# One PSUM bank for a head's sum and its transpose, and separate buffers for the two parts of the transposed weights

## The chip, the cores and the metric

The kernel runs on one core of one Trainium2 chip. The core has five engines with an instruction stream each: TensorE (PE in the rows; its weight loads are listed apart as PEld), VectorE (DVE), ScalarE (ACT), GpSimd (POOL) and SyncE (SP), which issues most of the transfers. An engine takes its instructions in the order in which they were laid down, and stands still where the next one waits for another engine. The metric is the device time of one execution in microseconds (us).

## The reference, cut to what matters

One layer of an encoder over 1024 tokens of width 1024: a norm, one input projection, two token mixers (retention in 8 heads, and sparse attention in 8 heads), an output projection with the residual, a gated per-layer embedding and a last norm. The change lies in the sparse attention, and in one place of the last stage that uses the same buffers. In the attention each token attends, per head, to the 256 keys that an indexer chose for it:

```python
    logits = (jnp.einsum('bthc,btkc->bthk', ql, c_sel)
              + jnp.einsum('bthr,btkr->bthk', qp, pe_sel)).astype(jnp.float32) * scale
    logits = jnp.where(sel_ok[:, :, None, :], logits, -jnp.inf)
    prob = jax.nn.softmax(logits, axis=-1).astype(c_kv.dtype)
    o_lat = jnp.einsum('bthk,btkc->bthc', prob, c_sel)
    return jnp.einsum('bthc,hcd->bthd', o_lat, w_uv)
```

The kernel doesn't gather. It computes the logits of all keys of a block, adds a bias that is hugely negative for keys not chosen, and multiplies the resulting weights with values projected beforehand (`VD`).

## The kernel before, in words

The attention works through blocks of 256 tokens, `i` = 3, 2, 1, 0, and in each block through 8 heads `h` (`attend`). A head of block `i` has 2i+2 key tiles of 128. Per head:

- **Logits** (L956, L957): two matmuls for each half of the tokens and each 512 keys go into a bank of the pair `lg`; VectorE adds the bias and takes the running maximum (L958), which releases that bank; ScalarE takes the exponential (L962). The result `lm` has tokens on the partitions.
- **Transposed weights** (`key_chunks`): for two key tiles at a time, three or four TensorE transposes (L979) put the weights, keys on the partitions now, into a bank of the pair `tp`. ScalarE copies them out rounded, the high part `th` (L985), and VectorE subtracts that from the bank, which leaves the low part `tl_` (L986). Both parts lie in one tile `t2`, of which there are two. So the copy of a chunk waits until the tile of the chunk two before it has no reader left, and its last reader is the last L1015 of that chunk.
- **The sum** (`by_dim`, blocks 3, 2 and 1): for each key tile one matmul with the high part (L1014) and one with the low part (L1015), all added up in a bank of the pair `oo`, of which they use the first 256 columns.
- **The transpose back**: ScalarE copies the sum out as `os` (L1017), TensorE transposes it in two halves (L1020) into the other bank of the pair `oo`, and VectorE reduces that into `od` (L1021). Since each head takes two banks of a pair, the sum of every head lies in the same bank, and its transpose in the other.

Block 0 takes another way (`by_token`, L989, L1003), which needs only the high part and one bank.

Beside the attention run, in blocks 3 and 2, the units of the retention (`retention_unit`: L836 to L842, L849 to L910), which share ScalarE, VectorE and TensorE, and in block 1 and later the output projection (`project`, L1106 to L1126) and the split of its weights (`prep_w`, L1061 to L1065: load, ScalarE copy, GpSimd subtract). The last stage (`tail_in`, `tail_out`) handles 128 tokens at a time; `tail_in` transposes the residual in two halves and splits it (L1186 to L1190), the second half into a tile of the tag `t2`.

The order of the instructions on each engine isn't that of the program. A planner lays it out when the program is built, by priorities (`high_priority`) and by its own estimate of when each instruction can start and when a buffer comes free. The same planner makes an instruction wait for whatever reader or writer of a reused tile came last.

Of the kernel before, what the change touches and what calls it, by code (L numbers as in the profile page):

```python
# [8 lines left out]
F32 = mybir.dt.float32  # L9
FR = mybir.dt.float32r  # L10
# [4 lines left out]
AF = mybir.ActivationFunctionType  # L15
OP = mybir.AluOpType
# [137 lines left out]
def _body(ctx, nc, tc, ap, dbg):  # L154
    V, A, G, T, Y = nc.vector, nc.scalar, nc.gpsimd, nc.tensor, nc.sync

    def f(t):
        return t.bitcast(F32)
# [17 lines left out]
    def pool(name, **kw):  # L176
        return tc.tile_pool(name=name, bufs=kw.pop("bufs", 1), reuse_waits="tile", **kw)
# [129 lines left out]
    for k in range(NT):  # L307
        hi, lo = w1[k]
# [21 lines left out]
    def rsqrt(out, ssum, n, w):  # L330
        a = tiny.tile([128, 16], F32, name="rs_a")[:, :w]
        y = tiny.tile([128, 16], F32, name="rs_y")[:, :w]
        z = tiny.tile([128, 16], F32, name="rs_z")[:, :w]
        first = V.tensor_scalar(a, ssum, 1.0 / n, EPS, op0=OP.mult, op1=OP.add)  # L334
        G.tensor_tensor(out=y, in0=a, in1=mhalf[:, :w], op=OP.pow)  # L335
        V.tensor_tensor(out=z, in0=y, in1=y, op=OP.mult)
        V.tensor_tensor(out=z, in0=z, in1=a, op=OP.mult)
        V.tensor_scalar(z, z, -0.5, 1.5, op0=OP.mult, op1=OP.add)
        return first, V.tensor_tensor(out=out, in0=y, in1=z, op=OP.mult)
# [255 lines left out]
    def bank(name):  # L595
        turns[name] += 1
        tags = places[name]
        return psC.tile([128, 512], F32, name=name, tag=tags[turns[name] % len(tags)])
# [194 lines left out]
    dq_ = ctx.enter_context(pool("dsaq", bufs=3))  # L793
# [120 lines left out]
    dw_ = dw_s.enter_context(pool("dsaw", side="right", bufs=2))  # L914
# [25 lines left out]
    def attend(i, h):  # L940
        q, od, den = blocks[i]
        q, ql = q[h]
        mxv = tiny.tile([128, 4], F32, name="mxv")
        pt = []
        for a in range(2):
            j = 2 * i + a
            w = 128 * (j + 1)
            tsl = slice(128 * a, 128 * a + 128)
            lm = dw_.tile([128, S], F32, name="lm", bufs=4)
            mx = mxv[:, a:a + 1]  # L950
            part = mxv[:, 2 + a:3 + a]
            for n, c0 in enumerate(range(0, w, 512)):
                c1 = min(w, c0 + 512)
                kk = KK[h][:, 512 * n:512 * n + 512]
                lg = lg_tile()[:, :c1 - c0]
                T.matmul(lg, q[:, tsl], kk[:, :c1 - c0], start=True, stop=False)  # L956
                T.matmul(lg, ql[:, tsl], kk[:, :c1 - c0], start=False, stop=True)  # L957
                V.tensor_tensor_reduce(out=lm[:, c0:c1], in0=lg, in1=bias[:, OFF[j] + c0:OFF[j] + c1], scale=1.0,  # L958
                                       scalar=-3.0e38 if c0 == 0 else part, op0=OP.add, op1=OP.max,
                                       accum_out=part if c1 < w else mx)  # L960
            V.tensor_scalar(mx, mx, -0.125, None, op0=OP.mult)  # L961
            A.activation(lm[:, :w], lm[:, :w], AF.Exp, bias=mx, scale=0.125, accum_out=den[:, a, h:h + 1])  # L962
            pt.append(lm)
        if i < 1:
            by_token(i, h, pt, od)
        else:
            by_dim(i, h, pt, od)

    def key_chunks(pt, s0, last, split):
        tp = bank("tp")  # L970
        cols = []
        o = 0
        for s in (s0, s0 + 1):
            ks_ = slice(128 * s, 128 * s + 128)
            c0 = o
            for a in range(2):
                if last and s == s0 + 1 and a == 0:
                    continue
                T.transpose(tp[:, o:o + 128], pt[a][:, ks_], ident)  # L979
                o += 128  # L980
            cols.append((s, c0, o))
        t2 = dw_.tile([128, 2, 512], FR, name="t2")
        th, tl_ = t2[:, 0], t2[:, 1]
        if split:
            A.activation(th[:, :o], tp[:, :o], AF.Copy)  # L985
            V.tensor_tensor(out=tl_[:, :o], in0=tp[:, :o], in1=f(th)[:, :o], op=OP.subtract)  # L986
        else:
            th = f(t2)[:, s0 // 2 % 2]
            A.activation(th[:, :o], tp[:, :o], AF.Copy)  # L989
        return [(s, c0, c1, th, tl_) for s, c0, c1 in cols]  # L990

    def by_token(i, h, pt, od):
        ot = bank("oo")[:, :256].rearrange("p (a c) -> p a c", a=2)
        cols = [x for s0 in range(0, 2 * i + 2, 2) for x in key_chunks(pt, s0, s0 == 2 * i, False)]
        for a in range(2):
            mms = []
            for s, c0, c1, th, tl_ in cols:
                if s > 2 * i + a:
                    continue
                c = slice(c1 - 256 + 128 * a, c1 - 128 + 128 * a)  # L1000
                mms += [(th[:, c], s)]
            for n, (t, s) in enumerate(mms):
                T.matmul(ot[:, a], t, f(VD[s])[:, h].rearrange("p l d -> p (l d)"), start=n == 0, stop=n == len(mms) - 1)  # L1003
        V.tensor_reduce(od[:, :, h], ot.rearrange("p a (l d) -> p a d l", l=2), AX.X, OP.add)

    def by_dim(i, h, pt, od):
        ot = bank("oo")[:, :256]
        n_s = 2 * i + 2
        for s0 in range(0, n_s, 2):
            for s, c0, c1, th, tl_ in key_chunks(pt, s0, s0 == 2 * i, True):  # L1010
                q0 = 256 - (c1 - c0)
                v2 = VD[s][:, h].rearrange("p l d -> p (l d)")
                end = s == n_s - 1
                T.matmul(ot[:, q0:], v2, th[:, c0:c1], start=s == 0, stop=False, skip_group_check=end)  # L1014
                T.matmul(ot[:, q0:], v2, tl_[:, c0:c1], start=False, stop=s >= n_s - 2, skip_group_check=end)  # L1015
        os_ = dw_.tile([128, 512], F32, name="os")[:, :256]
        A.activation(os_, ot, AF.Copy)  # L1017
        tbp = bank("oo").rearrange("p (j d) -> p j d", d=128)
        for a in range(2):
            T.transpose(tbp[:, a], os_[:, 128 * a:128 * a + 128], ident)  # L1020
        V.tensor_reduce(od[:, :, h], tbp[:, 0:2].rearrange("p j (l d) -> p j d l", l=2), AX.X, OP.add)  # L1021
# [146 lines left out]
    def tail_in(j):  # L1168
        xt = dw_.tile([128, D], F32, name="xt", tag="lm", bufs=4)
        Y.dma_start(xt, d_xb[j])  # L1170
        sq = dw_.tile([128, D], F32, name="sqx", tag="od")
        s1 = tiny.tile([128, 1], F32, name="s1")
        A.activation(sq, xt, AF.Square, accum_out=s1)
        r1 = tiny.tile([128, 1], F32, name="r1")
        rsqrt(r1, s1, D, 1)
        V.tensor_scalar(r1, r1, 0.5, None, op0=OP.mult)
        pr = rp_.tile([128, 2, 128], F32, name="pr", tag="gt")
        Y.dma_start(pr, ap["pT"][:, 128 * j:128 * j + 128].rearrange("(k p) t -> p k t", p=128))
        p2 = rp_.tile([128, 2, 2, 128], FR, name="p2", tag="og")
        A.activation(p2[:, 0], pr, AF.Copy)  # L1180
        G.tensor_tensor(out=p2[:, 1], in0=pr, in1=f(p2)[:, 0], op=OP.subtract)
        hi, lo = [], []
        for q in range(2):
            pt = bank("tp")
            for k in range(4):
                T.transpose(pt[:, 128 * k:128 * k + 128], xt[:, 512 * q + 128 * k:512 * q + 128 * k + 128], ident)  # L1186
            x2 = (dw_.tile([128, 2, 512], FR, name="xT", tag="t2") if q else
                  dq_.tile([128, 2, 512], FR, name="xT", tag="ql"))
            A.activation(x2[:, 0], pt, AF.Copy)
            V.tensor_tensor(out=x2[:, 1], in0=pt, in1=f(x2)[:, 0], op=OP.subtract)  # L1190
            for k in range(4):
                hi.append(x2[:, 0, 128 * k:128 * k + 128])
                lo.append(x2[:, 1, 128 * k:128 * k + 128])
        return xt, sq, r1, p2, hi, lo

    def per_layer(p2):
# [5 lines left out]
    def tail_out(j, xt, sq, r1, p2, hi, lo):  # L1202
# [33 lines left out]
        for eng, c in ((A, slice(0, 512)), (Y, slice(512, 1024))):  # L1236
            eng.dma_start(ap["out"][128 * j:128 * j + 128, c], xt[:, c])

    ready = tail_in(order[0])
    for n, j in enumerate(order):  # L1240
        after = tail_in(order[n + 1]) if n + 1 < NT else None
        tail_out(j, *ready)
        ready = after
# [16 lines left out]
```

## Time and profile before

| | |
|---|---|
| median of 3 runs | 807.86 us (806.78 to 809.04) |
| the profiled execution's own time | 805.41 us |
| its span, first to last instruction | 803.6 us |
| mean granted TensorE clock | 0.979 of full speed |
| busy: PE, DVE, ACT, POOL | 754.4, 582.0, 469.4, 311.9 us |

The span and the engines' times are those of one profiled execution; what lies around the span in it is 805.41 - 803.6 = 1.8 us. The attention with the retention beside it runs from about 395 to 522 us after the span's start, the attention with the projection beside it from there to about 640 us, and the last stage to the end.

### The profile page before, as it was taken

How to read it: one execution, taken by the hardware profiler on the slowest of the kernel's cores; microseconds unless marked ns; L12 is line 12 of the kernel's file. 1: busy time of each engine (PE TensorE's matmuls, PEld its weight loads, DVE VectorE, ACT ScalarE, POOL GpSimd, SP SyncE). 2: the span in 40 equal slices, each digit the busy share in tenths (PEclk: the TensorE clock that was granted, in tenths of full speed). 3: DMA queues.
4: the chain of work that ended last, by engine and by line, in shares of the span. 5: the costliest groups of instructions: out<-in, count | busy, mean ns of one | idle time of the engine just before them, and what ended most of it. 6: DMA issues, size and time to landing. Idle time of an engine off the chain costs nothing.

```text
span 803.6 us, 12584 instructions
## 1 busy us (share of the span) xinstructions
PE 754.4 (94%) x4415; PEld 656.1 (82%) x4415; DVE 582.0 (72%) x1254; ACT 469.4 (58%) x1025; POOL 311.9 (39%) x237
## 2 busy tenths in 40 slices
PE   9999699989999999998999989799999899999995
PEld 6888599879888887997888879588788687888885
DVE  4968489999997999999879778755754633255344
ACT  6543466729997899963756656744754321333232
POOL 2918325455666434710046557630312230411000
PEclk9999899999999999999999999999999999999998
DMA  9414815323333224604525454654533662131201
GB/s 317 122 28 127 240 48 131 91 55 94 117 117 119 80 66 135 210 28 131 131 66 153 159 150 115 207 174 108 178 123 91 220 211 95 61 112 66 79 26 53
DMA packets 60831, 97.11 MB, mean 121 GB/s; under 512 B 5376, under 2 KB 32384, under 8 KB 60768
## 3 DMA queue, kind: packets, MB, share of 16 engines
q1 hardware_dynamic: 57152, 89.76, 36.5%
q10 hardware_dynamic: 3616, 6.55, 2.3%
q8 instruction: 35, 0.57, 0.3%
q14 instruction: 28, 0.23, 0.1%
HBM read 67.06 MB, written 29.23 MB: 120 GB/s over the span
## 4 chain that ended last, share of the span: by engine, by line
PE 53%; DVE 20%; issue 11%; DMA 7%; POOL 4%; ACT 3%; SPq 2%; POOLq 0%; ACTq 0%; DVEq 0%
PE lg L1165 6%; PE ra L1165 5%; PE big L326 3%; PE big L325 3%; PE big L324 3%; PE oo L1165 3%; DVE res L657 3%; PE nb L502 2%; PE nb L503 2%; PE nb L504 2%; DMA qk<-d_f 2%; PE ra L1122 2%; PE ra L1123 2%; PE ra L1124 2%; DVE sc L484 2%
## 5 line engine op out<-in xcount | busy, mean ns | idle before, releaser
L237 POOL TENSOR_TENSOR wlo<-wraw,whi 128x512 fp32r<-128x512 f32 (+1 forms) x58 | 88.8, 1547 | 66.2 <-ACT whi L236 66.2
L673 ACT ACTIVATE ajunk<-key,cthr 128x1024 bf16<-128x1024 int16 (+5 forms) x96 | 95.5, 994 | 14.8 <-DVE key L634 10.5
L502 PE MATMUL nb<-whi,xhi 128*128 128x256 f32 x256 | 74.8, 295 | 8.8 <-ACT nst L506 8.8
L657 DVE TENSOR_SCALAR_CACHE_REDUCE res<-key,athr 128x384 f32<-128x384 int16 (+5 forms) x96 | 75.5, 786 | 2.1
L503 PE MATMUL nb<-wlo,xhi 128*128 128x256 f32 x256 | 74.1, 291 | 0.7 <-POOL wlo L237 0.7
L504 PE MATMUL nb<-whi,xlo 128*128 128x256 f32 x256 | 73.5, 290 | 0.0
L335 POOL TENSOR_TENSOR rs_y<-rs_a,mhalf 128x1 f32<-128x1 f32 (+1 forms) x26 | 26.2, 1006 | 101.5 <-DVE rs_a L334 98.7
L962 ACT ACTIVATE lm<-lm,mxv 128x896 f32<-128x896 f32 (+3 forms) x64 | 49.5, 775 | 25.6 <-DVE mxv L961 25.4
L985 ACT ACTIVATE t<-tp 128x512 fp32r<-128x512 f32 (+1 forms) x72 | 39.3, 556 | 39.5 <-PE oo L1015 27.1
L502 PEld LDWEIGHTS nb<-whi,xhi 128*128 128x128 f32 x256 | 50.7, 199 | 10.8 <-ACT nst L506 9.7
L325 PE MATMUL big<-xlo,whi 128*128 128x512 f32 x144 | 56.1, 389 | 0.0
L324 PE MATMUL big<-xhi,whi 128*128 128x512 f32 x144 | 55.7, 389 | 0.0
L986 DVE TENSOR_TENSOR t<-tp,t 128x512 fp32r<-128x512 f32 (+1 forms) x72 | 45.6, 640 | 14.0 <-ACT t L985 13.6
L326 PE MATMUL big<-xhi,wlo 128*128 128x512 f32 x144 | 55.7, 390 | 0.0
L484 DVE SCALAR_TENSOR_TENSOR sc<-rel,wi,sc 128x1024 f32<-128x1024 f32 (+5 forms) x42 | 51.0, 1213 | 5.8 <-ACT rel L480 3.1
L958 DVE CUSTOM_DVE_ANT_0 lm<-lg,bias 128x512 f32<-128x512 f32 (+2 forms) x64 | 36.7, 587 | 23.5 <-PE tp L979 12.0
L503 PEld LDWEIGHTS nb<-wlo,xhi 128*128 128x128 f32 x256 | 50.8, 199 | 1.9 <-POOL wlo L237 1.3
L504 PEld LDWEIGHTS nb<-whi,xlo 128*128 128x128 f32 x256 | 50.4, 198 | 0.6
L979 PE MATMUL tp<-cst,lm 128*128 128x128 f32 x288 | 48.1, 277 | 0.6 <-DVE rs_a L334 0.3
L1014 PE MATMUL oo<-t,vd 128*128 128x256 f32 (+1 forms) x144 | 40.5, 293 | 7.7 <-ACT os L1017 6.2
L1219 DVE SCALAR_TENSOR_TENSOR sqx<-sqx,oo 128x512 f32<-128x512 f32 (+1 forms) x17 | 10.5, 653 | 49.6 <-PE oo L1165 35.0
L236 ACT ACTIVATE whi<-wraw 128x512 fp32r<-128x512 f32 (+1 forms) x58 | 34.9, 609 | 14.9 <-POOL cg L535 4.2
(492 smaller groups left out, 2423.5 us busy)
## 6 DMA issues: line engine op xcount, KB each, us to landing
wraw<-in_w_t SPq DMA_DIRECT2D x26, 256.0 KB, 2.7
wraw<-in_w_n SPq DMA_DIRECT2D x24, 256.0 KB, 2.6
d_f<-o SPq DMA_DIRECT2D x8, 512.0 KB, 3.9
qk<-d_f SPq DMA_DIRECT2D x8, 512.0 KB, 4.5
ql<-d_qs SPq DMA_DIRECT2D x16, 256.0 KB, 5.1
qh<-d_qs SPq DMA_DIRECT2D x32, 128.0 KB, 4.1
twr<-in_w_out SPq DMA_DIRECT2D x8, 512.0 KB, 5.4
xt<-in_x SPq DMA_DIRECT2D x8, 512.0 KB, 3.5
```

The costliest lines, as they stand in the source:

```text
L237: G.tensor_tensor(out=lo, in0=raw, in1=f(hi), op=OP.subtract)
L324: T.matmul(outs[h], wh, xhi[k][:, sl], start=k == 0, stop=False)
L325: T.matmul(outs[h], wh, xlo[k][:, sl], start=False, stop=False)
L326: last = T.matmul(outs[h], wl, xhi[k][:, sl], start=False, stop=k == 7)
L484: V.scalar_tensor_tensor(dst, rel[:, :w], wi[:, i, h:h + 1], dst, op0=OP.mult, op1=OP.add)
L502: T.matmul(pb[:, a % 2], xhi[k][:, tsl], wh, start=k == 0, stop=False)
L503: T.matmul(pb[:, a % 2], xhi[k][:, tsl], wl, start=False, stop=False)
L504: last = T.matmul(pb[:, a % 2], xlo[k][:, tsl], wh, start=False, stop=k == 7)
L657: V.tensor_scalar(junk, src[:, KS[i]], thr[:, n:n + 1], 0.0, op0=op, op1=OP.add, accum_out=cnt[:, n:n + 1])
L673: A.activation(junk[:, :128 * (i + 1)], src[:, KS[i]], AF.Sign, bias=self.thr[:, n:n + 1], accum_out=cnt[:, n:n + 1])
L962: A.activation(lm[:, :w], lm[:, :w], AF.Exp, bias=mx, scale=0.125, accum_out=den[:, a, h:h + 1])
L1165: T.matmul(po[c.start // 512][:, c.start % 512:c.start % 512 + c.stop - c.start], a, b[:, c], start=k == 0 and m == 0, stop=k == n - 1 and ...
```

## The change

A head's sum and its transpose now lie in the two halves of one bank, so that successive heads take turns in the two banks of the pair `oo`. The tile `t2` becomes two: `th`, of which there are three, and `tl`, of which there are two. The tile `os` has half its size. The space per partition stays the same: t2 2 x 4 KB and os 2 x 2 KB were 12 KB; th 3 x 2 KB, tl 2 x 2 KB and os 2 x 1 KB are 12 KB. In the last stage the second half of the transposed residual takes its tiles from the tags `th` and `tl`. No computation is added or removed.

```diff
@@ key_chunks
-        t2 = dw_.tile([128, 2, 512], FR, name="t2")
-        th, tl_ = t2[:, 0], t2[:, 1]
+        th = tl_ = dw_.tile([128, 512], FR, name="th", bufs=3)
         if split:
+            tl_ = dw_.tile([128, 512], FR, name="tl")
             A.activation(th[:, :o], tp[:, :o], AF.Copy)
             V.tensor_tensor(out=tl_[:, :o], in0=tp[:, :o], in1=f(th)[:, :o], op=OP.subtract)
         else:
-            th = f(t2)[:, s0 // 2 % 2]
+            th = f(th)
             A.activation(th[:, :o], tp[:, :o], AF.Copy)
@@ by_dim
-        ot = bank("oo")[:, :256]
+        both = bank("oo")
+        ot = both[:, :256]
...
-        os_ = dw_.tile([128, 512], F32, name="os")[:, :256]
+        os_ = dw_.tile([128, 256], F32, name="os")
         A.activation(os_, ot, AF.Copy)
-        tbp = bank("oo").rearrange("p (j d) -> p j d", d=128)
+        tbp = both[:, 256:].rearrange("p (j d) -> p j d", d=128)
@@ tail_in
-            x2 = (dw_.tile([128, 2, 512], FR, name="xT", tag="t2") if q else
-                  dq_.tile([128, 2, 512], FR, name="xT", tag="ql"))
-            A.activation(x2[:, 0], pt, AF.Copy)
-            V.tensor_tensor(out=x2[:, 1], in0=pt, in1=f(x2)[:, 0], op=OP.subtract)
+            if q:
+                xh, xl = (dw_.tile([128, 512], FR, name="xT" + tag, tag=tag, bufs=n) for tag, n in (("th", 3), ("tl", 2)))
+            else:
+                x2 = dq_.tile([128, 2, 512], FR, name="xT", tag="ql")
+                xh, xl = x2[:, 0], x2[:, 1]
+            A.activation(xh, pt, AF.Copy)
+            V.tensor_tensor(out=xl, in0=pt, in1=f(xh), op=OP.subtract)
...
```

## Rows read from the trace of the kernel before

**Rows 1.** Busy time of each engine in three stretches: the attention beside the retention, the attention beside the projection, the last stage. Columns: stretch and its length, then busy us (and instructions) of PE, PEld, DVE, ACT and POOL, the granted clock, the DMA share, GB/s.
```profile
395.00:522.00 127.00, 112.85 (x820) 101.61 (x819) 103.02 (x262) 81.10 (x154) 70.80 (x67) 0.96 0.46 139
522.00:640.00 118.00, 113.16 (x695) 98.07 (x693) 67.25 (x206) 58.04 (x144) 24.56 (x16) 1.00 0.47 147
640.00:803.00 163.00, 154.26 (x714) 126.24 (x714) 66.54 (x169) 51.43 (x101) 30.62 (x30) 0.97 0.26 91
```

**Rows 2.** What TensorE's matmuls waited for between 355 and 645 us: who, for whom, us in total, times, the longest.
```profile
PE oo L1014 <- ACT os L1017: 6.2, 4, 3.2
PE lg L956 <- DVE mxv L958: 4.1, 5, 1.7
...
PE oo L1014 <- ACT t L985: 1.3, 2, 1.0
```

**Rows 3.** The instructions of the copy out, of the transpose back and of the reduction: count, then least, median and greatest ns of one, first and last start.
```profile
L1017 ACT ACTIVATE os<-oo x24: 373/379/388, 411.3 to 603.5; 128x256 f32<-128x256 f32 x24
...
L1020 PE MATMUL oo<-cst,os x48: 270/272/421, 412.8 to 608.1; 128*128 128x128 f32 x48
...
L1021 DVE TENSOR_REDUCE od<-oo x24: 407/416/426, 413.4 to 608.6; 128x128 f32<-128x256 f32 x24
```

**Rows 4.** The first of TensorE's four waits for `os`, in order of time: start, us, engine, line, operation; in brackets the idle time before it and who ended it.
```profile
407.58 0.59 ACT L985 ACTIVATE t<-tp 128x512 fp32r<-128x512 f32 x1
...
408.78 0.68 DVE L986 TENSOR_TENSOR t<-tp,t 128x512 fp32r<-128x512 f32 x1
...
410.82 0.60 ACT L985 ACTIVATE t<-tp 128x512 fp32r<-128x512 f32 x1
...
411.31 0.38 ACT L1017 ACTIVATE os<-oo 128x256 f32<-128x256 f32 x1
...
411.74 0.39 PE L1014 MATMUL oo<-t,vd 128*128 128x256 f32 x1 [1.51 <-ACT os L1017]
...
412.76 0.63 PE L1020 MATMUL oo<-cst,os 128*128 128x128 f32 x2
```

**Rows 5.** The second of them, the same way.
```profile
473.08 0.58 ACT L985 ACTIVATE t<-tp 128x512 fp32r<-128x512 f32 x1
...
473.55 0.38 ACT L1017 ACTIVATE os<-oo 128x256 f32<-128x256 f32 x1
...
473.99 0.39 PE L1014 MATMUL oo<-t,vd 128*128 128x256 f32 x1 [0.90 <-ACT os L1017]
...
474.68 0.38 PE L1020 MATMUL oo<-cst,os 128*128 128x128 f32 x2
```

**Rows 6.** The third of them.
```profile
509.69 0.58 ACT L985 ACTIVATE t<-tp 128x512 fp32r<-128x512 f32 x1
...
510.16 0.37 ACT L1017 ACTIVATE os<-oo 128x256 f32<-128x256 f32 x1
...
510.59 0.38 PE L1014 MATMUL oo<-t,vd 128*128 128x256 f32 x1 [0.61 <-ACT os L1017]
...
511.29 0.38 PE L1020 MATMUL oo<-cst,os 128*128 128x128 f32 x2
```

**Rows 7.** The fourth and longest, with what ScalarE did ahead of it.
```profile
516.52 1.06 ACT L1064 ACTIVATE wo3h<-twr 128x1024 fp32r<-128x1024 f32 x1 [2.89 <-DMA twr<-in_w_out]
517.48 0.58 ACT L985 ACTIVATE t<-tp 128x512 fp32r<-128x512 f32 x1
...
517.96 0.38 ACT L1017 ACTIVATE os<-oo 128x256 f32<-128x256 f32 x1
...
518.39 0.58 PE L1014 MATMUL oo<-t,vd 128*128 128x256 f32 x1 [3.22 <-ACT os L1017]
...
519.62 0.63 PE L1020 MATMUL oo<-cst,os 128*128 128x128 f32 x2
```

**Rows 8.** Stretches of 2 us around the first and the fourth of these waits; columns as in rows 1, the clock third from the end.
```profile
410.00:412.00 2.00, 0.49 (x5) 0.26 (x3) 1.79 (x2) 1.95 (x5) 2.00 (x2) 1.00 0.00 0
412.00:414.00 2.00, 2.00 (x11) 2.00 (x11) 1.46 (x5) 1.80 (x4) 1.04 (x1) 0.51 0.00 0
414.00:416.00 2.00, 2.00 (x14) 2.00 (x13) 1.42 (x5) 0.00 (x0) 0.51 (x2) 0.64 0.00 0
...
516.00:518.00 2.00, 0.00 (x0) 0.00 (x0) 0.00 (x0) 1.48 (x3) 0.35 (x1) 0.96 1.07 389
518.00:520.00 2.00, 1.61 (x8) 1.61 (x8) 1.11 (x4) 2.00 (x5) 2.00 (x1) 0.50 0.59 195
520.00:522.00 2.00, 2.00 (x13) 1.70 (x12) 1.28 (x4) 2.00 (x5) 1.75 (x2) 0.69 0.84 265
```

**Rows 9.** Waits of ScalarE and VectorE for the split of the transposed weights, between 395 and 522 us.
```profile
ACT t L985 <- PE oo L1015: 10.6, 9, 3.1
...
DVE t L986 <- ACT t L985: 3.9, 2, 2.4
```

**Rows 10.** The first of these waits between 522 and 582 us.
```profile
ACT t L985 <- PE oo L1015: 16.0, 8, 5.2
```

**Rows 11.** The latest reduction of a head against the sums that follow: the reduction of one head, the copy of the next head's sum, and the first matmul of the head after that.
```profile
590.91 0.43 DVE L1021 TENSOR_REDUCE od<-oo 128x128 f32<-128x256 f32 x1 [3.28 <-PE oo L1020]
591.04 0.38 ACT L1017 ACTIVATE os<-oo 128x256 f32<-128x256 f32 x1
...
594.80 0.29 PE L1014 MATMUL oo<-t,vd 128*128 128x256 f32 x1
```

More of the change, by code (lines that the diff above doesn't have):

```diff
@@ L1186, in tail_in @@
                 T.transpose(pt[:, 128 * k:128 * k + 128], xt[:, 512 * q + 128 * k:512 * q + 128 * k + 128], ident)
-            x2 = (dw_.tile([128, 2, 512], FR, name="xT", tag="t2") if q else
-                  dq_.tile([128, 2, 512], FR, name="xT", tag="ql"))
-            A.activation(x2[:, 0], pt, AF.Copy)
-            V.tensor_tensor(out=x2[:, 1], in0=pt, in1=f(x2)[:, 0], op=OP.subtract)
+            if q:
[5 more added lines that the diff above has]
+            V.tensor_tensor(out=xl, in0=pt, in1=f(xh), op=OP.subtract)
             for k in range(4):
-                hi.append(x2[:, 0, 128 * k:128 * k + 128])
-                lo.append(x2[:, 1, 128 * k:128 * k + 128])
+                hi.append(xh[:, 128 * k:128 * k + 128])
+                lo.append(xl[:, 128 * k:128 * k + 128])
         return xt, sq, r1, p2, hi, lo
```

## The prediction, made before the changed kernel was run

> **What bounds the kernel now.** I read the busy times by stage first. In all three stages that the change touches, TensorE is the engine that is nearly always busy: 112.85 of 127 us beside the retention, 113.16 of 118 beside the projection, 154.26 of 163 in the last stage [rows 1]. VectorE comes second, and only in the first of them is it close: 103.02 of 127. So a gain must come out of TensorE's idle time, and 127 - 112.85 = 14.2 us of it lie in the first stage. Next I read what TensorE waited for. The largest entry is the wait for `os`: 6.2 us in four waits, the longest 3.2; the waits for VectorE's logits follow with 4.1, and those for the high part `th` with 1.3 [rows 2]. The four waits are all in the first stage, and each has the same shape [rows 4 to 7]: TensorE has finished the sum of one head and stands at the first L1014 of the next, which can't write since ScalarE has not yet copied the old sum out of the one bank that all sums use. ScalarE is late not because the copy is long (379 ns) [rows 3] but because it stands behind other work in ScalarE's stream; in the fourth case behind a weight copy that itself waited 2.89 us for its load [rows 7].
>
> **The change part by part.** No instruction is added, removed or made longer: the copy still reads 128x256, the transposes and the reduction are the same. Only waits change, and then the order that the planner makes of them. The sum is in these steps.
>
> *The bank.* The next head's sum now has the other bank, so its L1014 no longer waits for `os`. But L1020, the transpose of the old head, still does, and in the present order it stands behind the first five matmuls of the next head. So the wait isn't gone; it moves to L1020, and to any L1014 whose `th` isn't ready, since `th` comes from the same ScalarE. I therefore price each of the four by when L1020 could start, with the order unchanged.
> - First [rows 4]: the inputs of the first four matmuls are there (`th` ended at 408.17, `tl` at 409.46). They run in the 1.51 us in which TensorE now idles. The fifth needs the `th` that ends at 411.42, L1020 the `os` that ends at 411.69. L1020 starts at about 411.75 and not at 412.76: 1.0 us.
> - Second [rows 5]: `th` ends at 473.66, `os` at 473.93; L1020 starts at 473.95 and not at 474.68: 0.7 us.
> - Third [rows 6]: `os` ends at 510.53; L1020 starts at about 510.6 and not at 511.29, but no more can be won than the 0.61 us of idle time: 0.6 us.
> - Fourth [rows 7]: `th` ends at 518.06, `os` at 518.34; L1020 starts at 518.4 and not at 519.62: 1.2 us. The rest of the 3.22 us stays, because ScalarE is still behind the weight copy.
>
> Together 1.0 + 0.7 + 0.6 + 1.2 = 3.5 us. From below: nothing, if each gain is taken back at the next wait for VectorE. From above: all 6.2 us, if the planner uses its freedom to put the stalled copies earlier.
>
> *The bank's release.* A bank is now held until VectorE's reduction of the head, not only until the copy, and the head after next needs it. The latest reduction ended at 591.34, and the first sum that would need that bank began at 594.80 [rows 11]: 3.5 us to spare, so I price it at nothing. If that cover goes, each head pays up to the reduction's 416 ns [rows 3] and its handover.
>
> *Three `th`, two `tl`.* ScalarE sat 10.6 us in nine waits for the last L1015 of an older chunk [rows 9]. With a third `th` it can copy one chunk further ahead, so most of these waits leave ScalarE. They don't vanish: `tl` still has two buffers, so VectorE's subtraction waits for the same L1015, and the bank in `tp` is not free before it. Behind it in VectorE's stream stand the logits L958, whose lateness TensorE already pays with 4.1 us [rows 2]. After the release only the subtraction (0.68 us) is left to do and not copy and subtraction (0.59 + 0.68) [rows 4], so a chunk is ready up to 0.6 us sooner. TensorE waited only 1.3 us for `th` in all [rows 2]. Bounds: a gain of these 1.3 us, and a loss of up to the whole 10.6 us if all of it reached TensorE through VectorE. I take 0: VectorE has 127 - 103.02 = 24 us of idle time there to absorb it [rows 1], and 3.9 us of it is already spent on waiting for this `th` [rows 9]. Between 522 and 582 us ScalarE sat another 16.0 us [rows 10], in the stage in which TensorE hardly idles [rows 1]; nothing is won or lost there.
>
> *Block 0, the last stage, `os`'s size.* Block 0 uses one bank per head as before. The last stage gets a third buffer for the high part of half its tiles, where TensorE is busy 154.26 of 163 us [rows 1]. Nothing, unless that cover goes.
>
> *The clock.* After the first wait the granted clock fell to 0.51 and 0.64 in two stretches of 2 us, after the fourth to 0.50 and 0.69 [rows 8]: 2.4 GHz became 1.2 for part of them. Lost: 2 x 0.49 + 2 x 0.36 = 1.7 us, and 1.61 x 0.50 + 2 x 0.31 = 1.4 us. Before both falls TensorE had been idle for the better part of a stretch [rows 8]. In the unchanged order some 2.7 us of the fourth idle time and 0.8 us of the first stay, so I leave both falls in the sum.
>
> The Trainium skill, "TensorE: Matmul & The Clock Gate", Part 1, says that throttled is the default state and that activity releases it. By that rule the first fall, whose idle time is broken up and shortened, would go as well, and the sum would be 3.5 + 1.7 = 5.2 us; by the rows it is 3.5.
>
> The profiled execution took 805.41 us, 1.8 us of it around the span of 803.6, and lies 2.45 us under the median of the runs, 807.86. Taken off each: 801.9 and **804.4 us**. What differs by under 0.3% (2.4 us) can't be told from no change.
>
> **The rivals.**
> - *More than the sum.* The planner, no longer held by the bank and by `t2`, lays `os` and `th` ahead of the weight copy. Then all 6.2 + 1.3 us of waits go, and with them both falls of the clock: 7.5 + 1.7 + 1.4 = 10.6 us, 797.3 us. For it: the planner decides by when a buffer is free, and that is what changes. Against it: it didn't foresee the 2.89 us load in front of the weight copy, and still won't.
> - *Nothing that can be told.* L1020 and its followers are earlier, but TensorE then waits the longer for VectorE's logits (4.1 us now), so that 2 to 3 of the 3.5 us are given back: 806 to 808 us. The third `th` does nothing either, since two banks in `tp` and two `tl` still limit the chunks in flight. For it: VectorE is busy 81% of that stage.
> - *Slower: the wait moves to VectorE.* What ScalarE sat out (10.6 us) VectorE sits out, with the logits behind it, and TensorE stands at L956. If two thirds reach TensorE, 7.1 - 3.5 = +3.6 us, 811.5 us; it ends slower by over 2.4 us from 5.9 of the 10.6 us on. For it: VectorE's stream is fuller than ScalarE's (103 against 81 us) [rows 1]. Against it: its 24 us of idle time.
> - *Slower: the bank's release.* If the planner lays reductions late, the head after next waits for each. At 0.42 us for the 22 heads that have one two before them, 9.2 - 3.5 = +5.7 us, 813.6 us. It decides from 5.9 us in all, 0.27 us a head. Against it: the 3.5 us to spare.
>
> The Trainium skill, "PSUM — Partial Sum Buffer", § PSUM bank collisions, wants engines kept apart by bank, not by address. By that rule a sum that shares a bank with a transpose stays locked until VectorE has read the transpose, the mechanism of this last rival; it would give 813.6 us, where rows 11 give 804.4.
>
> **How the numbers follow.** Forecast (gain 2.4 to 5.2 us, 802.7 to 805.4): 0.35. More: 0.15. Nothing: 0.28. VectorE: 0.17. Bank: 0.05. So faster 0.35 + 0.15 = 0.50, the same 0.28, slower 0.22. The range runs from 797.5, which leaves out the far half of the second case, to 812, which leaves out the bank's rival and the far end of VectorE's: about 2 in 10 in all. The forecast's own range is 802.7 to 805.4. The largest thing that I can't see is the planner: every order after the first changed tile can shift, on SyncE's and GpSimd's queues too (the loads of `qk` and of the weights, the weight splits), and one new stall like the fourth with its fall of the clock costs 3.2 + 1.4 = 4.6 us, which alone would turn the forecast.
>
> **What would show it.** Right: the entry L1014 for `os` gone from TensorE's waits, a smaller one of L1020 for `os` in its place; ScalarE's 10.6 us for L1015 down to 3 or less, and a new wait of VectorE's L986 for L1015; TensorE's idle time in that stage down by 3 to 4 us from 14.2; the last stage equally long. Wrong: TensorE's wait for the logits (L956) grown by 5 us or more, a new wait of L1014 for the reduction L1021, a fall of the clock at a place where there was none, or a stage other than this one that changes its length by over 2 us.

## The result, and the profile after

The changed kernel takes 796.14 us (median of 4 runs, 792.77 to 798.29) where the kernel before took 807.32 beside it: a ratio of 0.985, interval [0.980, 0.990]. That is 11.2 us less, three times the 3.5 us of the sum, and 1.4 us below the foot of the range. A few executions of the kernels in this document were disturbed and took far longer; the medians and ratios leave them out, and a dash in the tables stands where the profiled execution was one of them.

The profiled execution took 798.29 us, the longest of its runs; its span is 796.1 us, 7.5 shorter than before. The busy times of the first stage, in the columns of [rows 1]:

```profile
395.00:522.00 127.00, 117.95 (x870) 107.89 (x870) 106.13 (x285) 87.97 (x169) 76.18 (x69) 0.97 0.50 152
```

Between 395 and 522 us TensorE executes 870 matmuls where it executed 820, and idles 9.1 us where it idled 14.2. Stretches bound to the work say more than stretches bound to the clock on the wall. From the first transposes of the weights (L979) to the last matmul of the retention (L893), before and after:

```profile
397.50:494.90 97.40, 89.31 (x672) 82.18 (x673) 80.24 (x195) 58.46 (x112) 52.28 (x55) 0.96 0.40 120
```

```profile
399.70:490.60 90.90, 86.37 (x673) 80.21 (x673) 77.96 (x196) 58.53 (x112) 52.49 (x56) 1.00 0.42 123
```

This part is 6.5 us shorter: 3.6 us less idle time, and a granted clock of 1.00 where it was 0.96. The clock's part of that isn't the change's alone: in a second profiled execution of the same changed kernel, 796.0 us long, the clock fell once in this part (0.50 and 0.65 between 414 and 418 us), and it took 92.4 us with a clock of 0.98. What TensorE waits for between 355 and 645 us, against [rows 2]:

```profile
PE ra L1123 <- DVE mTl L1114: 3.3, 1, 3.3
PE oo L1015 <- ACT th L985: 3.3, 3, 2.1
...
PE lg L956 <- DVE mxv L958: 0.4, 1, 0.4
```

The wait for `os`, 6.2 us, is gone without a remainder: no L1021 (the transpose back, L1020 before) waits for it either. The wait for the logits fell from 4.1 to 0.4 us, which nothing in the sum foresaw. How a head's end looks now (start, us, engine, line; the copy out is L1018, the reduction L1022):

```profile
471.74 0.39 ACT L1018 ACTIVATE os<-oo 128x256 f32<-128x256 f32 x1
...
472.25 0.28 PE L1015 MATMUL oo<-th,vd 128*128 128x256 f32 x1
...
472.54 1.10 PE L854 MATMUL ra<-vt,kt 128*128 128x128 f32 x8
...
474.20 0.38 PE L1021 MATMUL oo<-cst,os 128*128 128x128 f32 x2
...
477.23 0.41 DVE L1022 TENSOR_REDUCE od<-oo 128x128 f32<-128x256 f32 x1
```

The copy ends at 472.13, and the transposes that need it are laid so far behind that TensorE reaches them at 474.20, after a stretch without a gap. In [rows 4 to 7] they came right behind five matmuls that themselves stood behind the copy. The order of the instructions has changed, not only the waits. This head is one of 24: from the end of the copy to the transposes it takes 0.05 to 6.1 us in the changed kernel, 0.27 to 6.5 us in the one before.

### The profile page after: what moved, and what is told of

It reads as the page before. It is cut to its first block, busy times and chain, and to the rows that moved or that the text cites. A ratio compares the mean times of both kernels' runs of the same rounds, so it can differ in the third digit from the quotient of the medians.

```text
span 796.1 us, 12587 instructions
## 1 busy us (share of the span) xinstructions
PE 751.8 (94%) x4415; PEld 655.7 (82%) x4415; DVE 580.5 (73%) x1254; ACT 469.1 (59%) x1025; POOL 312.2 (39%) x237
## 4 chain that ended last, share of the span: by engine, by line
PE 60%; DVE 21%; DMA 8%; issue 4%; ACT 3%; SPq 1%; POOL 1%; ACTq 0%; POOLq 0%; DVEq 0%
PE lg L1166 6%; DVE res L657 5%; PE ra L1166 5%; PE ra L1125 3%; PE ra L1123 3%; PE ra L1124 3%; PE oo L1166 3%; DMA qk<-d_f 2%; PE tp L979 2%; PE nb L502 2%; PE nb L503 2%; PE nb L504 2%; DVE sc L484 2%; PE ra L893 1%; PE lg L956 1%
## 5 line engine op out<-in xcount | busy, mean ns | idle before, releaser
L985 ACT ACTIVATE th<-tp 128x512 fp32r<-128x512 f32 (+1 forms) x72 | 39.8, 557 | 39.8 <-PE tp L979 38.5
L335 POOL TENSOR_TENSOR rs_y<-rs_a,mhalf 128x1 f32<-128x1 f32 (+1 forms) x26 | 28.0, 1076 | 86.7 <-DVE rs_a L334 83.7
L502 PEld LDWEIGHTS nb<-whi,xhi 128*128 128x128 f32 x256 | 50.4, 198 | 10.9 <-ACT nst L506 9.7
L986 DVE TENSOR_TENSOR tl<-tp,th 128x512 fp32r<-128x512 f32 (+1 forms) x72 | 45.7, 639 | 5.9 <-ACT th L985 3.4
L979 PE MATMUL tp<-cst,lm 128*128 128x128 f32 x288 | 48.2, 277 | 0.3 <-DVE tl L986 0.3
L1015 PE MATMUL oo<-th,vd 128*128 128x256 f32 (+1 forms) x144 | 41.4, 296 | 3.3 <-ACT th L985 3.3
L236 ACT ACTIVATE whi<-wraw 128x512 fp32r<-128x512 f32 (+1 forms) x58 | 34.9, 609 | 15.2 <-POOL cg L535 5.0
L1016 PE MATMUL oo<-tl,vd 128*128 128x256 f32 (+1 forms) x144 | 40.3, 313 | 0.1
```

The source lines that it names most:

```text
L502: T.matmul(pb[:, a % 2], xhi[k][:, tsl], wh, start=k == 0, stop=False)
```

## The experiments

Three theories to begin with: **A**, the bank does it; **B**, the third `th` does it; **C**, neither by itself, but the order that the planner lays around them. In the tables, "idle + clock" is worked out from stretches of 2 us, from the first L979 to the end of the span: TensorE's idle time, plus its busy time times one minus the granted clock, summed. Each figure is from one profiled execution; the changed kernel's two agree. For the kernel before the sum is 28.3 + 6.1 = 34.4 us, for the changed one 22.8 + 4.4 = 27.2.

**Halves of the change.** The whole again; the bank alone (buffers as before); the buffers alone (two banks a head as before); the whole with two `th`.

```diff
 e1_bank_only, against the kernel before
-        ot = bank("oo")[:, :256]
+        both = bank("oo")
+        ot = both[:, :256]
-        tbp = bank("oo").rearrange("p (j d) -> p j d", d=128)
+        tbp = both[:, 256:].rearrange("p (j d) -> p j d", d=128)
 e2_buffers_only, against the changed kernel
-        both = bank("oo")
-        ot = both[:, :256]
+        ot = bank("oo")[:, :256]
-        tbp = both[:, 256:].rearrange("p (j d) -> p j d", d=128)
+        tbp = bank("oo").rearrange("p (j d) -> p j d", d=128)
 e3_two_th, against the changed kernel
-        th = tl_ = dw_.tile([128, 512], FR, name="th", bufs=3)
+        th = tl_ = dw_.tile([128, 512], FR, name="th", bufs=2)
```

> The changed kernel once more, beside the three kernels that take it apart. All theories: 0.985 of the kernel before, 793 to 798 us.

> The kernel before with the bank's half of the change alone: sum and transpose in one bank, heads taking turns; t2 and os as before. Theory A (the bank is the cause: the sum of the next head no longer waits for os, and the falls of the clock behind these waits go too): 10 of the 11 us, 0.985 to 0.988 of before. Theory B (the third th is the cause, since it frees ScalarE of its waits for old chunks): 0.998 to 1.002. Theory C (the planner's new order is the cause, whichever tile triggers it): no value foretold, anything from 0.98 to 1.01, and not near the sum of the parts.

> The other half alone: th (three), tl (two) and the small os, but the sum and its transpose in two banks as before. Theory A: 0.997 to 1.002, with TensorE's wait for os still there (6 us or more). Theory B: 0.985 to 0.988. Theory C: anything from 0.98 to 1.01; the shortfalls of the two halves don't add up to that of the whole.

> The whole change but with two th and not three: the parts are still released apart, th after the last matmul that reads it and not after the last of tl. Theory A: 0.985 to 0.988, as the whole. Theory B: 0.995 to 1.000, ScalarE's wait for old matmuls back at 8 us or more between 395 and 522 us. Theory C: a value of its own.

| kernel | median us | ratio to before, interval | idle + clock, us |
|---|---|---|---|
| the whole again | 796.88 | 0.983 [0.980, 0.986] | 27.2 |
| bank alone | 787.10 | 0.973 [0.970, 0.977] | 19.2 |
| buffers alone | 796.91 | 0.986 [0.982, 0.989] | 27.8 |
| whole, two `th` | 790.21 | 0.975 [0.972, 0.978] | – |

Either half alone gives as much as the whole or more, and taking the third `th` away makes the whole faster. Two gains that simply add up can't do that, so neither A nor B explains the table. Whether ScalarE's waits came back with two `th`, the sign that B had named, can't be said, since that row has a dash. The buffers alone leave both banks as they were, and yet TensorE's wait for `os` at the sum, which only the bank was to remove, fell from 6.2 to 1.8 us (buffers alone, 395 to 650 us):

```profile
PE lg L956 <- DVE mxv L958: 2.5, 5, 0.6
PE oo L1014 <- ACT os L1017: 1.8, 2, 1.4
```

**The order held.** To part the waits from the order, a program is built twice: once for the tiles whose order is wanted, once for the tiles to be tried, and the second build is made to keep every engine's order of the first. Only the order of issue is added, no semaphore. In the traces of both kernels that are held to the order of before, TensorE's 4415 matmuls follow one another exactly as in the kernel before.

```diff
+    for engine, line in follow.items():            # order of the first build, engine by engine
+        for p, q in zip(line, line[1:]):
+            tc.add_manual_dep(ins[q], names[p], mybir.DependencyInfo(
+                mybir.DependencyClass.NoSync, mybir.DependencyReason.DATA), reason="order of issue")
```

> The bank's half of the change alone, but with the order of the instructions on every engine held to that which the planner laid down for the kernel before. What differs from the kernel before is then only which waits there are. Theory W (the waits themselves are the cause, falls of the clock included): 0.975 to 0.985 of before, as with the order of its own (0.973). Theory O (the planner's new order is the cause): no more than the 3.5 us that the prediction worked out for the unchanged order, 0.995 to 1.000.

> All buffers of the changed kernel, order of the instructions on every engine held to that of the kernel before. Theory W: 0.980 to 0.987, as with the order of its own. Theory O: 0.993 to 1.000, little apart from the same run with the bank alone, since VectorE takes over ScalarE's waits in the old order.

> All buffers of the changed kernel, order held to that which the planner laid down for the bank alone (0.973). It tells whether the third th itself costs the 1% that the whole change lies behind the bank alone. Theory O: 0.970 to 0.975, the buffers cost nothing and only the planner's other order did. Theory W: 0.980 to 0.985, the third th moves waits to VectorE whatever the order.

| tiles | order laid for | median us | ratio, interval | idle + clock, us |
|---|---|---|---|---|
| bank alone | before | 804.57 | 0.996 [0.993, 0.999] | 31.7 |
| whole change | before | 807.33 | 0.999 [0.996, 1.002] | 34.8 |
| whole change | bank alone | 788.55 | 0.974 [0.971, 0.977] | – |

The first line is the experiment that the prediction's sum describes: the bank with the order unchanged. It gives 0.996, or 3.2 us; the sum said 3.5, and the interval runs from 1.0 to 5.5 us. At the first stall its trace does what [rows 4] was argued to become. ScalarE and TensorE at the first stall (bank, old order; here L1025 and L1026 are the sum, L1028 the copy, L1031 the transposes):

```profile
411.86 0.37 PE L1025 MATMUL oo<-t,vd 128*128 128x256 f32 x1
...
412.06 0.28 PE L1026 MATMUL oo<-t,vd 128*128 128x256 f32 x1
412.18 0.29 PE L1025 MATMUL oo<-t,vd 128*128 128x256 f32 x1
412.31 0.28 PE L1026 MATMUL oo<-t,vd 128*128 128x256 f32 x1
412.67 0.60 ACT L995 ACTIVATE t<-tp 128x512 fp32r<-128x512 f32 x1
413.17 0.38 ACT L1028 ACTIVATE os<-oo 128x256 f32<-128x256 f32 x1
413.32 0.38 PE L1025 MATMUL oo<-t,vd 128*128 128x256 f32 x1 [0.74 <-ACT t L995]
...
413.60 0.44 PE L1031 MATMUL oo<-cst,os 128*128 128x128 f32 x2
```

Four matmuls of the next head run before the copy, the fifth waits 0.74 us for `t` where [rows 4] have 1.51 for `os`, and the transposes start at 413.60, right after the copy's end at 413.55. The transposes of the weights that stand ahead of the stall begin at 409.61 in the kernel before and at 411.47 here; counted from them, 413.60 corresponds to 411.74, and the prediction said 411.75. The clock holds in the stretches around it (columns of [rows 1]):

```profile
412.00:414.00 2.00, 1.26 (x9) 0.78 (x8) 1.94 (x2) 1.93 (x5) 2.00 (x2) 1.00 0.00 0
414.00:416.00 2.00, 2.00 (x18) 2.00 (x18) 1.93 (x8) 1.68 (x3) 0.91 (x1) 1.00 0.00 0
```

At the other three stalls the transposes come as promptly, 0.05, 0.06 and 0.16 us after the copy's end, but not all of it is kept. The second stall's 0.90 us are gone, and 4 us later TensorE waits 0.68 us longer for the high part than before. First the kernel before, then the bank with the old order:

```profile
478.39 0.38 PE L1014 MATMUL oo<-t,vd 128*128 128x256 f32 x1 [1.04 <-ACT t L985]
```

```profile
478.40 0.39 PE L1025 MATMUL oo<-t,vd 128*128 128x256 f32 x1 [1.72 <-ACT t L995]
```

The fourth wait is 3.23 us long where it was 3.22, behind a weight copy that starts 1.45 us later. Over all of it the wait changes its name and keeps most of its length (bank, old order, 395 to 650 us):

```profile
PE oo L1025 <- ACT t L995: 5.9, 4, 3.2
PE lg L961 <- DVE mxv L963: 4.7, 6, 1.7
```

The second line of the table adds the separate buffers, and nothing is gained; the difference to the first line lies within the intervals. In that kernel ScalarE's waits for the readers of an old chunk, 27.1 us between 395 and 640 us before the change, are gone; it waits for the transposes instead, and VectorE's subtraction has one wait of 5.1 us for a sum that it did not have:

```profile
ACT th L995 <- PE tp L984: 33.4, 18, 5.6
```

```profile
DVE tl L996 <- PE oo L1026: 5.1, 1, 5.1
```

So the freedom is there and is worth nothing while the order stays. The third line gives the whole change the order that was laid for the bank alone, and it is then as fast as the bank alone: the third `th` costs nothing by itself, and neither does the holding of an order. For the change as it is built, with the planner's numbers as they are, that settles C over A and B for all that lies beyond the bank's 3 us.

**Parts of the order, and the banks' alternation.** Bank's tiles with only TensorE's order held to the old one; old tiles with only ScalarE's and VectorE's orders held to the bank's; and the whole change with every head in the same bank, so that its sum has to wait for the last head's reduction. The old tiles under the bank's whole order were not tried: a sum would stand ahead of the copy that it waits for.

```diff
 e5_one_bank, against the changed kernel
-        both = bank("oo")
+        both = psC.tile([128, 512], F32, name="oo", tag=places["oo"][0])
 e11_bank_old_pe: the loop above for ("PE",) of the old order, tiles of the bank alone
 e10_old_tiles_bank_act_dve: for ("Activation", "DVE") of the bank's order, tiles as before
```

> The bank alone; TensorE's order held to that of the kernel before, the rest laid down by the planner anew. If TensorE's order carries the gain: 0.994 to 1.000, as with all orders held. If ScalarE's or VectorE's order carries it: 0.975 to 0.985.

> The buffers of the kernel before, nothing of the change; ScalarE's and VectorE's order held to that which the planner laid down for the bank alone, the other engines' orders laid down by the planner anew around it. Theory D (the order of before is simply a poor one, and a better one doesn't need the bank): 0.973 to 0.985. Theory N (the good orders need the second bank for the sums): 0.995 or more.

> The whole change, but every head uses the same bank for both halves, so that each sum must wait until VectorE has reduced the head before. If the release by the reduction were dear (the prediction's last rival), this doubles it: 22 heads by 0.4 us and more, 1.00 to 1.02 of before. If the planner finds an order around it, 0.98 to 0.99, with waits of L1015 for L1022 in TensorE's list.

| kernel | median us | ratio, interval | idle + clock, us |
|---|---|---|---|
| bank, TensorE's old order | 804.97 | 0.999 [0.997, 1.002] | 29.5 |
| old tiles, bank's ScalarE and VectorE | 804.95 | 0.997 [0.996, 0.999] | 31.2 |
| whole, every head the same bank | 810.00 | 1.003 [1.000, 1.005] | 37.3 |

For the whole time a part of the order is worth nearly nothing, whichever part. But where it is lost differs. With the old tiles and the bank's order of ScalarE and VectorE, the stretch from the first transposes of the weights to the last retention matmul takes 90.2 us at a clock of 1.00, no more than the 90.9 us of the changed kernel. What is won there is lost behind it, above all in one wait for the copies of `mT` (395 to 650 us):

```profile
400.90:491.10 90.20, 85.68 (x672) 79.44 (x673) 79.17 (x195) 57.90 (x110) 53.11 (x55) 1.00 0.42 124
```

```profile
PE ra L1134 <- DVE mTl L1125: 5.2, 1, 5.2
```

So, by this one trace, the shorter stage beside the retention needs neither the bank nor the third `th`, only another order. With TensorE's order held to the old one nothing is gained, the result that had been named for the case that TensorE's order carries the gain; it doesn't tell that from a gain that needs all the orders together. With one bank for all heads the gain is gone, but not by a wait of the sum for the reduction, which the trace doesn't have. In the order that is laid for these tiles TensorE waits for the release of the transposes' bank and for loads instead:

```profile
PE tp L979 <- DVE tl L986: 5.4, 5, 2.2
PE ra L1110 <- DMA mr<-d_mix: 3.8, 3, 2.6
```

**Another plan for the same tiles.** If an order is worth 2%, is this change's order its own, or the luck of one draw? A number that has nothing to do with the change, the priority of the retention's units, makes the planner lay other orders. It is 900 in the kernel; 300 and 0 were run for each set of tiles.

```diff
-            with tc.high_priority(900):
+            with tc.high_priority(300):   # or 0
```

> The kernel before with one number of the planner changed (the priority of the retention's units, 900 to 300), which gives it another order and nothing else. Theory D (orders scatter, and that of before is a poor draw): anything from 0.975 to 1.01, more likely below 0.997. Theory N: 0.997 to 1.01.

> The bank alone with the same number changed. Theory N: 0.97 to 0.98, still 2 to 3% below the run with the old buffers and the same number. Theory D: on either side of that run, within 1.5% of it.

> The kernel before with the retention's unit given priority 0 instead of 900, so that the planner lays another order on all engines. Theory S (the bank shortens the attention beside the retention whatever plan is laid): TensorE's idle time and clock lost in that stage stay at 10 us or more, as in every plan seen so far without the bank's order. Theory D (only the draw of plans): they may fall to 5 us as well. The time of the whole says little on either: 800 to 815 us.

> The same priority 0 with the bank's half alone. Theory S: idle time and clock lost beside the retention 3 to 6 us, at least 5 below the kernel with the old buffers and the same priority. Theory D: within 3 us of it, either way.

> The whole change with priority 300. Theory S: idle time and clock lost beside the retention 3 to 6 us, against 10.8 with the old buffers and this priority; the whole at 790 to 804 us, since the stages behind it scatter by 6 us from plan to plan. Theory D: 8 us or more beside the retention.

> The whole change with the retention's unit at priority 0. Theory S (the change brings its gain under any plan): 0.986 times the kernel before, as at 900 and 300, or less, 790 to 797 us, and idle time and clock lost beside the retention below the old buffers' 7.7 us. Theory D (the change is one draw of plans among others): the ratio lies anywhere in the 0.973 to 0.998 seen, no nearer to 0.986 than to the old buffers' 0.991 under this priority.

> The separate buffers alone (two banks a head as before) with priority 300. At 900 they gave 0.9855. Theory S for this half: 0.986 again, near 796 us. Theory D: anywhere between 0.973 and 0.998; with no bank to help, nearest to the old buffers' 0.9976.

> The separate buffers alone with priority 0. Theory S for this half: below the old buffers' 0.991 by about 0.01, near 792 us. Theory D: within 0.005 of 0.991 or above it.

Ratio to the kernel before with its interval, and idle + clock in us:

| tiles | priority 900 | 300 | 0 | mean ratio |
|---|---|---|---|---|
| as before | 1; 34.4 | 0.998 [0.995, 1.000]; 32.5 | 0.991 [0.988, 0.994]; 30.4 | 0.996 |
| bank alone | 0.973 [0.970, 0.977]; 19.2 | 0.997 [0.995, 0.998]; 31.9 | 0.992 [0.989, 0.996]; 27.4 | 0.987 |
| buffers alone | 0.986 [0.982, 0.989]; 27.8 | 0.986 [0.981, 0.991]; 24.5 | 0.985 [0.980, 0.990]; 24.7 | 0.985 |
| whole change | 0.985 and 0.983; 27.2 | 0.986 [0.981, 0.990]; 22.9 | 0.977 [0.972, 0.982]; 21.2 | 0.982 |

Read by columns: with the same number, the whole change is ahead of the old tiles by 1.5 to 1.7, 1.2 and 1.4%. In these three plans, at least, its gain isn't the luck of one. Read by rows: the old tiles win 0.9% by a number alone, and the bank alone, the best of all at 900, has nothing over the old tiles at 300 and 0 that the intervals can tell. Its 787.1 us, the fastest median measured here, is a draw of the plan; the two other plans give it nothing. So theory N, that the good orders need the second bank, fell too: it asked for 0.97 to 0.98 at 300. (At 0 the profiled execution of the bank was its fastest, 794.97 us against a median of 800.85; its 27.4 us are low for that kernel.) The buffers alone are ahead in all three columns, by 1.4, 1.2 and 0.6%; the last falls between what S and D (only the draw of plans) expected, and the intervals there still touch. Theory S, that the bank shortens the attention beside the retention under any plan, fell: at 0 the old tiles lose 7.7 us there, not 10 or more, and the bank's 5.7 are 2 us better, not 5. At 300 the bank has 3.4 us there against 10.9, and loses it behind that stage. For the whole change S held: beside the retention it loses 4.5 us (6.2 in the second execution), 6.0 and 2.7 where the old tiles lose 11.3, 10.9 and 7.7.

What stays the same over the three plans, with the old tiles and with the whole change, is ScalarE's wait (395 to 640 us; line numbers differ, the first is the kernel before at 900, the second the changed one):

```profile
ACT t L985 <- PE oo L1015: 27.1, 18, 5.2
```

```profile
ACT th L985 <- PE tp L979: 38.5, 29, 4.9
...
ACT th L985 <- PE oo L1015: 0.9, 2, 0.8
```

With the old tiles ScalarE waits 27.1, 35.3 and 34.9 us for the readers of an old chunk, with the whole change 0.9, 0.9 and 0.6. The buffers alone have none, 1.5 and none, the bank alone 10.4, 24.5 and 27.5. The sets without the wait gain under all three numbers, and the bank alone gains only under the plan that brings its wait down. Yet removing the wait alone, in the old order, gave nothing, and the old tiles had a short stage beside the retention with it. So the likeliest reading is that the gain lies in what the planner does once it needn't reckon with that wait. That is argued and not shown, and which of the planner's moves carries the gain was not isolated.

Why the best and the worst plan of the bank differ is seen in TensorE's waits at the hand-over to the projection. At 300:

```profile
PE ra L1121 <- DMA mr<-d_mix: 5.2, 2, 3.4
PE ra L1134 <- ACT mTh L1124: 3.8, 1, 3.8
```

At 900 (bank alone):

```profile
PE oo L1015 <- ACT t L985: 2.8, 2, 1.9
...
PE ra L1123 <- DVE mTl L1114: 0.8, 1, 0.8
...
PE ra L1110 <- DMA mr<-d_mix: 0.3, 1, 0.3
```

Neither the loads of `mr` nor the copies of `mT` use the bank; the same tiles under two plans have them late or in time. The changed kernel has such a place too, 3.3 us for `mTl` behind two VectorE operations that were laid ahead of it:

```profile
627.13 3.43 DVE L1033 TENSOR_TENSOR od<-od,gd 128x512 f32<-128x512 f32 x2
630.49 0.68 DVE L1114 TENSOR_TENSOR mTl<-ra,mTh 128x512 fp32r<-128x512 f32 x1
...
631.22 0.80 PE L1123 MATMUL ra<-wo0h,mTh 128*128 128x512 f32 x1 [3.33 <-DVE mTl L1114]
```

## Why the prediction was wrong

- **The step that failed** is the clause "with the order unchanged". It was written as the condition of the sum, and the sum was then taken for the kernel. Held to that order the bank gives 3.2 us; the kernel as it is built gives 11.2. With the whole change held to it, 0.999, nothing is gained that can be told. The planner stood in the text as "the largest thing that I can't see", with a price for a new stall (4.6 us) and, for a gain, only the single move of the rival "more than the sum". A better order of everything else had no price.
- **The bank's 3.5 us** were near in size (3.2, between 1.0 and 5.5) and right in mechanism where the transposes are concerned: at all four stalls they start at the copy's end. But the terms don't add up one by one as the sum has them: the second's 0.7 us are given back at the next wait for `th`, which the text had only as its lower bound, there for VectorE; the fourth's wait is no shorter; and part of what is gained is clock, which the sum left out. The kernel as built has another order: the head shown has its transposes 2 us behind the copy.
- **The clock.** Both falls were left in the sum. In the held order the first is gone: where [rows 8] have 0.51 and 0.64 the stretches shown above have 1.00, though 0.74 us of idle time stay. The Trainium skill, "TensorE: Matmul & The Clock Gate", Part 1, holds that activity releases the throttle; by that rule the first fall was to go, and here the trace agrees with the Trainium skill and not with my reading of the rows. In the changed kernel's two executions a wait of 0.91 us at this place has no fall behind it, one of 1.41 us has one to 0.50. The 1.7 us did not reach the time by themselves: a new fall at 504 us (1.6) and a longer one behind the fourth wait (2.6 for 1.4) took the place of the first and of one at 640 us (clock lost in all, 6.1 us before, 5.7 in the held order). The text also missed a fall as large as the first: between 480 and 484 us the clock before was 0.57 in both stretches, 1.7 us lost behind the wait at 478.39. It isn't in the changed kernel.
- **Three `th`.** "Most of these waits leave ScalarE" is right. That VectorE would sit them out is right only in the old order (5.1 us) and with one bank; in the changed kernel no such wait is among VectorE's, though the buffers alone have 4.0 us of it in seven waits and the whole change at 300 has 4.3 us in one. Nothing, the price that I took, is what the buffers give with the order held (0.999 against 0.996). As built they are worth 0.6 to 1.4%.
- **The bank's release** shows up in no wait of a sum for a reduction, not even with one bank for all heads. What it costs through the planner is another matter: with one bank the gain is gone. The Trainium skill, "PSUM — Partial Sum Buffer", § PSUM bank collisions, wants engines kept apart by bank, not by address; the wait that I worked out from it is in none of these traces.
- **The rival "more than the sum"** comes nearest with 797.3 us, but its way is not the one taken. It had a chance of 0.15, and that its size came out is luck. The planner did not lay `th` ahead of every weight copy; a stall of that kind is still there, with a fall of the clock:

```profile
500.03 1.06 ACT L1065 ACTIVATE wo1h<-twr 128x1024 fp32r<-128x1024 f32 x1 [2.29 <-DMA twr<-in_w_out]
...
501.52 0.58 PE L1015 MATMUL oo<-th,vd 128*128 128x256 f32 x1 [2.06 <-ACT th L985]
```

- **What would show it.** The entry for `os` is gone as foretold, and ScalarE's 10.6 us for L1015 are down to under 1; but no smaller wait of L1021 for `os` stands in its place, and no wait of VectorE for that matmul. The idle time of the first stage fell by 5.1 us, not 3 to 4; the logits' wait shrank where I had only asked whether it would grow; from the last retention matmul to the first of the last stage it is 136.6 us long and not 142.1, a sign that I had named as one against me. That mark has moved with the order, ahead of matmuls of the projection: behind it the kernel is 2.3 us longer (168.9 and not 166.6), so 3.2 of the 5.5 us are won.

## What to carry to other kernels

Where a planner lays the order, a sum "with the order unchanged" prices a kernel that will not be built: give the new order a range of its own, on both sides. How wide can be measured before the change is judged: change a number that has nothing to do with it and see how far the time moves (here 0.9% with the old tiles, 2.3% with the bank). Compare two sets of buffers under several such plans, since the one that wins under one plan, here the bank alone, may have nothing under the next.

## What the runs showed of the hardware

The price of a stall is not its length. The wait of 3.2 us behind a weight copy cost 1.4 us of clock in the kernel before [rows 7, 8]. In the bank's kernel with the old order it is 3.23 us long at the same place and costs 0.2 + 1.0 + 1.0 + 0.4 = 2.6 us:

```profile
518.00:520.00 2.00, 0.43 (x2) 0.43 (x3) 0.45 (x1) 2.00 (x4) 0.89 (x1) 0.50 1.00 370
520.00:522.00 2.00, 2.00 (x9) 1.70 (x9) 1.60 (x6) 2.00 (x5) 1.75 (x2) 0.50 0.45 149
522.00:524.00 2.00, 2.00 (x9) 1.81 (x8) 1.21 (x6) 2.00 (x5) 2.00 (x1) 0.50 0.93 251
524.00:526.00 2.00, 2.00 (x16) 2.00 (x15) 0.89 (x3) 1.08 (x3) 2.00 (x2) 0.80 0.77 226
```

And in the changed kernel a shorter one, 2.06 us, costs 0.1 + 1.0 + 1.0 + 0.9 = 3.0 us:

```profile
500.00:502.00 2.00, 0.48 (x2) 0.48 (x3) 0.63 (x3) 1.97 (x3) 0.94 (x2) 0.73 0.54 204
502.00:504.00 2.00, 2.00 (x10) 1.70 (x10) 1.09 (x6) 1.59 (x4) 2.00 (x2) 0.50 1.00 339
504.00:506.00 2.00, 2.00 (x9) 1.78 (x8) 0.53 (x3) 1.66 (x5) 2.00 (x2) 0.50 0.00 0
506.00:508.00 2.00, 2.00 (x11) 1.92 (x10) 1.64 (x4) 1.38 (x3) 2.00 (x2) 0.56 0.54 170
```

The changed kernel's second execution has the same stall, 1.92 us long, and pays 0.6 + 1.0 + 0.1 = 1.7 us:

```profile
502.00:504.00 2.00, 1.90 (x9) 1.72 (x10) 1.59 (x6) 2.00 (x5) 2.00 (x1) 0.68 1.04 357
504.00:506.00 2.00, 2.00 (x10) 1.86 (x9) 0.45 (x3) 1.66 (x5) 2.00 (x3) 0.50 0.32 123
506.00:508.00 2.00, 1.99 (x15) 1.66 (x14) 2.00 (x7) 1.69 (x4) 2.00 (x2) 0.96 0.55 172
```

So the price of one stall in one kernel differs by 1.3 us from one execution to the next, and a fall priced from a single trace is uncertain by as much.

By this profile TensorE's time outside idle time and clock is no constant either: from the first L979 to the end, with the same matmuls, it is 371.7 us in the kernel before, 369.2 in the changed one (369.8 in its second execution), and 365.8 to 372.1 over all orders run. So 2.5 of the 9.7 us by which that stretch is shorter lie in neither; why the same matmuls take less in one order than in another was not looked into.
